# Weight sums pinned to the output projections, and the down projection's seven products in another order

## The chip, the cores and the metric

The kernel runs on one core of one Trainium2 chip. The metric is the device time of one execution in microseconds (us). The engines are TensorE (PE; its weight loads are shown apart as PEld), VectorE (DVE), ScalarE (ACT), GpSimd (POOL) and SyncE (SP). DMA transfers are issued on the queues of SP, ACT and POOL and move through 16 DMA engines that all of them use.

## What is computed

One layer of a streaming encoder on a sequence of 1024 tokens of width 1024, in float32: stick-breaking attention with 16 heads, cross-attention of 4 heads into 256 memory rows, and a gated MLP of width 2816 with a causal convolution over three tokens. Each of the three ends in a projection, a residual and a layer norm:

```python
h = layer_norm(DN_ALPHA * h + mixer(h) @ mix_wo, ln_g[0], ln_b[0])
h = layer_norm(DN_ALPHA * h + mem_cross_attn(h, mem, xa_wq, xa_wkv, xa_wo), ln_g[1], ln_b[1])
# conv_ffn: u = conv(h @ w_up) + b;  g, val = split(u);  (gelu(g) * val) @ w_down
h = layer_norm(DN_ALPHA * h + conv_ffn(h, ffn_up, ffn_conv, ffn_conv_b, ffn_down), ln_g[2], ln_b[2])
```

## The kernel before

Every float32 product is made of three matmuls on operands that are split into a high and a low part (`split`, lines 77 to 87: a cast for the high part, a subtraction for the low one; `mm3`, lines 100 to 103: the three matmuls). A stage's instructions are written in an order, but a scheduler that simulates the program puts each engine's queue into its final order: an instruction that is ready early and has nothing before it in its way can move far to the front of its engine's queue. The queues themselves are then served strictly in order.

The stages are: loading x and projecting the first head (lines 384 to 408), attention head by head with the projections of the next head mixed in (`proj_steps`, `attention`; at the end the keys and values of the memory, `mem_steps`), the first output projection with its layer norm in eight token blocks (`out_ln`, from line 463), cross-attention, the second output projection in the same way, the MLP's up projection with convolution and gate in 22 steps (`late`, `stage1` to `stage3`), and the down projection with the last layer norm (from line 810). In the first stage, `qk_out` (lines 131 to 140) builds head 0's q and k; four transfers q<-q on SP copy halves of q into the tile that the second matmul of the scores, line 216, reads.

Both products of the MLP use a Strassen-like scheme: each operand is cut into 2 x 2 blocks, and seven products of sums of blocks take the place of eight. For the down projection four sums of weight blocks are needed, u1 to u4, each of 11 tiles of 256 KB. They are built in DRAM by transfers alone (`u_steps`, lines 419 to 428): 44 plain copies on SP's queue (line 422) and 44 accumulating transfers on POOL's queue (line 426). The stage's text calls this generator six times after each token block of the first output projection, and six times before each block of the second. Nothing but the copies' own data order holds these transfers to that place. In the projections, the loads of a token block (attention output or h, and the residual) are issued on ACT's queue, a block ahead; SP's queue has the stores of h1 or h2 there (`h_d<-r`, line 488) and loads for what follows. The layer norm's power -0.5 is an instruction on POOL (line 446) between two parts of the norm on DVE.

The last up-projection pair ends with two gates that are stored to DRAM on SP's queue (`gated`, line 738). The down projection loads four quarter tiles ("slots") for each of 11 steps from there (`slot`, line 825, 44 loads `float<-g_d`; two of the eleven steps need the last two gates), and a weight block for each step (`w_block`, line 835). Its products are named 1, 6, 2, 7, 5, 4 and a last one. Each of the first six has 11 steps of 12 matmuls into four PSUM banks; two sets of four banks alternate, so that DVE or ACT empties one while PE fills the other. Sums of slots are made on DVE between the steps. The last product runs row block by row block, 33 matmuls each, and after each of its four blocks two layer norms are done (`finish`), that of a row block in the upper half and that of one in the lower half of the tokens. `layer_norm` has two forms: one on DVE alone, and a spread one (argument `spread`) that uses ACT for the scaling, POOL for the gain and DVE for the offset.

Of the kernel before, what the change touches and what calls it, by code (L numbers as in the profile page):

```python
# [41 lines left out]
def trunk(ctx, tc, out, xT, xn, memT, wqk, wv, wo, xq, xk, xv, xo, up, cw, dn, lng, lnb):  # L42
# [395 lines left out]
    def layer_norm(r, g, b, spread=False):  # L438
        st = smallp.tile([P, 2, 6], F32, name="st")
        for c in range(2):  # L440
            nc.vector.bn_stats(out=st[:, c], in_=r[c])
# [287 lines left out]
    def gated(w, c):  # L729
# [80 lines left out]
    plan = {1: (0, "11"), 6: (0, "u2"), 2: (2, "21"), 7: (None, "u3"), 5: (1, "u1"), 4: (3, "u4")}  # L810
    with ExitStack() as c4:
# [40 lines left out]
        def add(d, x, y):  # L852
            nc.vector.tensor_tensor(out=d, in0=x, in1=y, op=ALU.add)

        def finish(i, spread):
            layer_norm((rs[i][:, 0:512], rs[i][:, 512:1024]), *gb, spread=spread)
# [4 lines left out]
        def factors(m, kt):  # L861

            s, n = plan[m]
            if m == 6:
                nc.vector.tensor_tensor(out=slot(kt, 0), in0=slot(kt, 1), in1=slot(kt, 0), op=ALU.subtract)
            if m == 7:
                x = ea.tile([P, 512], F32, name="sum", bufs=2)
                nc.vector.scalar_tensor_tensor(out=x, in0=slot(kt, 0), scalar=-1.0, in1=slot(kt, 3),
                                               op0=ALU.mult, op1=ALU.subtract)
            else:  # L870
                x = slot(kt, s)
            w = w_block(n, kt)
            a = ea.tile([P, 2, 512], R, name="aop", bufs=4)
            if kt % 2 == 0:
                two["w"] = whlp.tile([P, 2, 2, 512], R, name="whl")
            return (x, (a[:, 0], a[:, 1])), (w, (two["w"][:, kt % 2, 0], two["w"][:, kt % 2, 1]))

        two = {}

        def down(bank, b, a, w, first, last, more):  # L880
# [3 lines left out]
        banks = ([f(name="ya") for f in (acc_tile, acc_tile, pv_tile, pv_tile)],  # L884
                 [f(name="yb") for f in (z_tile, z_tile, tp_tile, tp_tile)])
        last_ops = [[None, None] for _ in range(NH)]
        gb = None
        for n, m in enumerate((1, 6, 2, 7, 5, 4)):
            y = banks[n % 2]
            more = m in (2, 7, 4)  # L890
            if m == 5:
                y = banks[0][:] = [f(name="ya") for f in (acc_tile, acc_tile, pv_tile, pv_tile)]
            for kt in range(NH):
                ops = factors(m, kt)
                for x, d in ops:
                    split(x, *d)
                a, w = ops[0][1], ops[1][1]
                for b in range(4):
                    down(y[b], b, a, w, kt == 0 and not more, kt == NH - 1, more)
                if m == 1:  # L900
                    nc.vector.tensor_tensor(out=slot(kt, 1), in0=slot(kt, 1), in1=slot(kt, 3), op=ALU.subtract)
                if m == 2:
                    add(slot(kt, 2), slot(kt, 2), slot(kt, 0))
                if m == 5:
                    t = w_block("22", kt)
                    wo = room(kt, 0, R), room(kt, 1, R)
                    split(t, *wo)
                    last_ops[kt][1] = wo
                    if 3 <= kt < 7:
                        residual("22", kt - 3, c22[kt - 3], ALU.subtract)  # L910
                if m == 4:
                    vo = room(kt, 3, R), room(kt - 1, 2, R) if kt else ea.tile([P, 512], R, name="vl")
                    split(slot(kt, 2), *vo)
                    last_ops[kt][0] = vo
                    if 3 <= kt < 7:
                        residual("21", kt - 3, c21[kt - 3])
                    elif kt >= 7:
                        residual("12", kt - 7, c12[kt - 7], ALU.subtract)
            if m == 7:
                gb = load_ln(ep, 2)  # L920
            for b in range(4):
                if m == 1:
                    nc.scalar.copy(out=c21[b], in_=y[b])
                elif m == 6:
                    add(c12[b], y[b], c21[b])
                elif m == 2:
                    residual("11", b, y[b])
                elif m == 7:
                    add(c22[b], y[b], c21[b])
                elif m == 5:  # L930
                    add(c22[b], c22[b], y[b])
# [47 lines left out]
```

## Time and profile before

| | us |
|---|---|
| median of 3 runs (1631.63 to 1636.67) | 1632.85 |
| the profiled execution | 1636.42 |
| its span, first to last instruction | 1634.6 |
| PE busy | 1520.0 (93%) |
| DVE busy | 1099.9 (67%) |
| ACT busy | 700.7 (43%) |
| POOL busy | 639.4 (39%) |

All times within the execution count from the span's start. A busy PE is one with a matmul in its pipeline, not one at its peak; the granted clock tells how fast it may run (1.00 is 2.4 GHz, 0.50 is 1.2 GHz). The DMA share is the mean busy share of the 16 DMA engines, and can come out a little over 1. A timeline line reads: start, duration, engine and line, operation, tile written <- tiles read, count, and in brackets the engine's idle time before it with what ended it.

### The profile page before, as it was taken

To read this page: it belongs to the slowest core of one execution; us is meant where nothing else is said; L and a number is where in the kernel's file an instruction comes from. 1 tells how busy PE (TensorE), PEld (TensorE's weight loads), DVE (VectorE), ACT (ScalarE), POOL (GpSimd) and SP (SyncE) were. 2 spreads that over 40 slices of the span, in tenths; PEclk is the share of its full clock that TensorE was granted. 3 is DMA by queue.
4 is the path that set the end of the run, shared out by engine and by line. 5 is a ranking of instruction groups with operands and counts; after the bars stand their busy time and mean duration, and the time that the engine had idled before them with its cause. 6 is when DMAs were issued, how large, how long until landed. Compare 5 with 4: busy or idle time off the path is not lost.

```text
span 1634.6 us, 20991 instructions
## 1 busy us (share of the span) xinstructions
PE 1520.0 (93%) x7508; PEld 1266.1 (77%) x7508; DVE 1099.9 (67%) x1500; ACT 700.7 (43%) x1306; POOL 639.4 (39%) x565
## 2 busy tenths in 40 slices
PE   5639999999998899999999987999999999799996
PEld 4428888888887698888888866788888888588875
DVE  2127566676667974655545789877777777868778
ACT  2315556555556651113332334444444444344551
POOL 4758656655655881035520133233232322000004
PEclk8759999999999999999999999999999999899998
DMA  9975221212223653433326412222222222854532
GB/s 276 258 183 127 71 62 51 76 53 59 65 62 109 194 195 101 133 112 109 110 68 190 142 52 80 91 78 77 80 93 86 78 90 78 283 182 129 187 103 104
DMA packets 99193, 191.01 MB, mean 117 GB/s; under 512 B 11408, under 2 KB 33040, under 8 KB 99088
## 3 DMA queue, kind: packets, MB, share of 16 engines
q1 hardware_dynamic: 84688, 160.30, 30.9%
q0 software_dynamic: 6336, 11.54, 4.0%
q10 hardware_dynamic: 8064, 17.83, 3.3%
q8 instruction: 59, 0.97, 0.2%
q14 instruction: 46, 0.38, 0.1%
HBM read 146.63 MB, written 57.67 MB: 125 GB/s over the span
## 4 chain that ended last, share of the span: by engine, by line
PE 76%; DMA 9%; DVE 9%; issue 2%; POOL 2%; ACT 2%; SPq 0%; DVEq 0%; POOLq 0%; ACTq 0%
DMA u_d<-in_dn 4%; PE yacc L101 4%; PE yacc L102 4%; PE yacc L103 4%; PE mb L101 3%; PE mb L103 3%; PE mb L102 3%; PE tp L231 3%; PE qkacc L101 3%; PE qkacc L102 3%; PE qkacc L103 3%; PE ma L101 2%; PE ma L102 2%; PE ma L103 2%; PE mc L101 2%
## 5 line engine op out<-in xcount | busy, mean ns | idle before, releaser
L222 DVE TENSOR_TENSOR_SCAN sig<-sig 128x896 f32<-128x896 f32 (+7 forms) x128 | 204.2, 1603 | 90.7 <-POOL sig L219 51.4
L87 POOL TENSOR_TENSOR whl<-wraw,whl 128x512 fp32r<-128x512 f32 (+2 forms) x97 | 178.5, 1856 | 155.9 <-ACT whl L79 154.7
L446 POOL TENSOR_TENSOR rs<-rs,mhalf 128x1 f32<-128x1 f32 x24 | 21.3, 890 | 362.4 <-DVE rs L445 362.4
L85 DVE TENSOR_TENSOR wT<-tp,wT 128x512 fp32r<-128x512 f32 (+1 forms) x160 | 99.0, 630 | 67.5 <-ACT wT L79 65.8
L79 ACT CAST wT<-tp 128x512 fp32r<-128x512 f32 (+1 forms) x160 | 86.4, 546 | 106.2 <-PE tp L231 101.4
L79 ACT CAST whl<-wraw 128x512 fp32r<-128x512 f32 (+3 forms) x113 | 82.2, 739 | 108.2 <-PE yacc L103 33.1
L217 ACT ACTIVATE sig<-z 128x384 f32<-128x384 f32 (+2 forms) x192 | 91.8, 495 | 81.6 <-PE z L216 80.8
L101 PE MATMUL qkacc<-xh,whl 128*128 128x512 f32 x256 | 104.9, 410 | 21.8 <-ACT xh L79 19.7
L101 PE MATMUL mb<-b_t,ws 128*128 128x512 f32 x264 | 105.1, 399 | 10.5 <-ACT ws L79 8.1
L103 PE MATMUL qkacc<-xh,whl 128*128 128x512 f32 x256 | 103.2, 403 | 4.6 <-POOL whl L87 4.6
L103 PE MATMUL mb<-b_t,ws 128*128 128x512 f32 x264 | 104.4, 396 | 0.0
L102 PE MATMUL mb<-b_t,ws 128*128 128x512 f32 x264 | 103.8, 393 | 0.0
L102 PE MATMUL qkacc<-xl,whl 128*128 128x512 f32 x256 | 103.7, 405 | 0.0
L219 POOL TENSOR_SCALAR_AFFINE_SELECT sig<-sig 128x128 f32<-128x128 f32 x128 | 58.0, 457 | 114.9 <-ACT sig L217 107.9
L102 PE MATMUL yacc<-wo,whl 128*128 128x512 f32 x256 | 100.9, 394 | 0.0
L103 PE MATMUL yacc<-wo,whl 128*128 128x512 f32 x256 | 100.8, 394 | 0.0
L101 PE MATMUL yacc<-wo,whl 128*128 128x512 f32 x256 | 100.4, 393 | 0.3 <-ACT whl L79 0.3
L216 PE MATMUL z<-k,q 128*128 128x384 f32 (+2 forms) x192 | 68.6, 359 | 31.1 <-DMA q<-q 31.1
L231 PE MATMUL tp<-ident,sig 128*128 128x128 f32 x576 | 89.0, 274 | 8.6 <-DVE wT L85 8.4
L79 ACT CAST ws<-wt 128x512 fp32r<-128x512 f32 x88 | 54.3, 620 | 94.7 <-PE mb L103 52.6
L83 POOL TENSOR_SCALAR whl<-wraw 128x512 fp32r<-128x512 f32 (+2 forms) x74 | 62.3, 871 | 79.8 <-PE q2acc L103 23.1
L85 DVE TENSOR_TENSOR whl<-wraw,whl 128x512 fp32r<-128x512 f32 (+3 forms) x90 | 66.4, 746 | 35.0 <-ACT whl L79 34.8
(225 smaller groups left out, 4435.0 us busy)
## 6 DMA issues: line engine op xcount, KB each, us to landing
u_d<-in_dn SPq DMA_DIRECT2D x44, 256.0 KB, 13.1
wraw<-in_up SPq DMA_DIRECT2D x22, 512.0 KB, 3.7
wr<-in_up SPq DMA_DIRECT2D x22, 512.0 KB, 3.5
g_d<-gate SPq DMA_DIRECT2D x22, 512.0 KB, 2.7
float<-g_d SPq DMA_DIRECT2D x44, 256.0 KB, 5.4
wraw<-u_d SPq DMA_DIRECT2D x44, 256.0 KB, 3.0
wraw<-in_dn SPq DMA_DIRECT2D x33, 256.0 KB, 3.1
q<-q SPq DMA_DIRECT2D x64, 128.0 KB, 2.5
```

The costliest lines, as they stand in the source:

```text
L79: nc.scalar.copy(out=hi, in_=src)
L83: nc.gpsimd.tensor_scalar(out=hi, in0=src, scalar1=1.0, scalar2=0.0, op0=ALU.mult, op1=ALU.add)
L85: nc.vector.tensor_tensor(out=lo, in0=src, in1=hi.bitcast(F32), op=ALU.subtract)
L87: nc.gpsimd.tensor_tensor(out=lo, in0=src, in1=hi.bitcast(F32), op=ALU.subtract)
L101: nc.tensor.matmul(o, lhsT=lh, rhs=rh, start=first, stop=False, skip_group_check=more)
L102: nc.tensor.matmul(o, lhsT=lh, rhs=rl, start=False, stop=False, skip_group_check=more)
L103: nc.tensor.matmul(o, lhsT=ll, rhs=rh, start=False, stop=last, skip_group_check=more)
L216: nc.tensor.matmul(z[:, :b - a], lhsT=q2[:, tb], rhs=k1[:, a:b], start=False, stop=True)
L217: nc.scalar.activation(out=sig[:, a:b], in_=z[:, :b - a], func=AF.Sigmoid, scale=-0.125)
L219: nc.gpsimd.affine_select(out=sig[:, S - P:S], in_=sig[:, S - P:S], pattern=[[-1, P]], base=-1, channel_multiplier=1, compare_op=ALU.is_ge ...
L222: nc.vector.tensor_tensor_scan(out=kr, data0=kr, data1=kr, initial=1.0, op0=ALU.mult, op1=ALU.bypass)
L231: nc.tensor.transpose(out=tp[:, k], in_=sigs[2 * d + u][:, P * j:P * j + P], identity=ident)
```

## The change

The 88 transfers that build the weight sums get an edge each to the instruction that was traced before them on their engine, so that the scheduler can't move them ahead of it. The store of the last pair's two gates goes to POOL's queue. The seven products of the down projection run in the order 1, 6, 5, 7, 4, 3 and last 2. The bank sets are 0, 1, 0, 1, 1, 0 and a new one for the last product; the statistics of each half row for the last layer norm are taken as soon as that half is complete (`whole`), and the layer norms of the lower half of the tokens are done during product 3, leaving four for the last product, all in the spread form.

```diff
     def u_steps():
         for n, x in (("u1", "11"), ("u3", "22"), ("u2", "22"), ("u4", "21")):
             for kt in range(NH):
-                nc.sync.dma_start(out=u_d[n][kt], in_=b_block(x, kt))
+                tc.keep_in_program_order(nc.sync.dma_start(out=u_d[n][kt], in_=b_block(x, kt)))
                 yield
         for n, x in (("u1", "12"), ("u3", "12"), ("u2", "u1"), ("u4", "u2")):
             for kt in range(NH):
-                nc.gpsimd.dma_start(out=u_d[n][kt], in_=u_d[x][kt] if x[0] == "u" else b_block(x, kt),
-                                    accum_op=ALU.add, max_dma_last_dim=2048)
+                tc.keep_in_program_order(nc.gpsimd.dma_start(
+                    out=u_d[n][kt], in_=u_d[x][kt] if x[0] == "u" else b_block(x, kt),
+                    accum_op=ALU.add, max_dma_last_dim=2048))
                 yield
...
-            nc.sync.dma_start(out=g_d[w.j + c], in_=gate[c])
+            (nc.gpsimd if w is pairs[-1] else nc.sync).dma_start(out=g_d[w.j + c], in_=gate[c])
...
-    plan = {1: (0, "11"), 6: (0, "u2"), 2: (2, "21"), 7: (None, "u3"), 5: (1, "u1"), 4: (3, "u4")}
+    plan = {1: (0, "11"), 6: (0, "u2"), 5: (1, "u1"), 7: (1, "u3"), 4: (3, "u4"), 3: (0, "22")}
...
+        def whole(n, b):
+
+            i, ns = rows(n)[b]
+            if i not in stats:
+                stats[i] = ep.tile([P, 2, 6], F32, name=f"st{i}")
+            nc.vector.bn_stats(out=stats[i][:, int(n[1]) - 1], in_=rs[i][:, ns])
...
+        for m, n in ((1, 0), (6, 1), (5, 0), (7, 1), (4, 1), (3, 0)):
+            if m in (1, 6, 5):
+                sets[n] = bank_set(n)
+            y, more = sets[n], m not in (1, 6, 5)
             for kt in range(NH):
...
+                elif m == 5:
+                    nc.vector.scalar_tensor_tensor(out=slot(kt, 1), in0=slot(kt, 0), scalar=-1.0, in1=slot(kt, 3),
+                                                   op0=ALU.mult, op1=ALU.subtract)
+                elif m == 7:
+                    plus(slot(kt, 0), slot(kt, 2), slot(kt, 0))
...
+                elif m == 3:
+                    last_ops[kt][0] = room(kt, 0, R), room(kt - 1, 2, R) if kt else ea.tile([P, 512], R, name="lo2")
+                    split(slot(kt, 2), *last_ops[kt][0])
+                    if kt < 4:
+                        residual("12", kt, c12[kt], ALU.subtract)
+                    if kt in (3, 5, 7, 9):
+                        finish(4 + (kt - 3) // 2, kt != 9)
...
+                elif m == 7:
+                    plus(c22[b], c22[b], y[b], ALU.subtract)
+                    whole("22", b)
+                elif m == 4:
+                    plus(c21[b], c21[b], y[b])
+                    whole("21", b)
                 else:
-                    add(c21[b], c21[b], y[b])
+                    plus(c12[b], c12[b], y[b])
+                    whole("12", b)
+        y = bank_set(1)
         for b in range(4):
             for kt in range(NH):
-                a, w = last_ops[kt]
-                down(banks[0][b], b, a, w, False, kt == NH - 1, True)
-            finish(4 + b, b < 3)
-            add(c12[b], c12[b], banks[0][b])
-            finish(b, b % 2 == 0)
+                down(y[b], b, *last_ops[kt], kt == 0, kt == NH - 1, False)
+            plus(c11[b], c11[b], y[b])
+            whole("11", b)
+            finish(b, True)
```

## Rows read from the trace of the kernel before

**Rows 1.** Table by stages: length, busy us of each engine, clock, DMA share, GB/s.

```profile
26.40:77.40 51.00, 32.06 (x107) 23.77 (x106) 5.53 (x8) 12.18 (x23) 31.07 (x36) 0.73 1.09 267
77.40:108.50 31.10, 0.03 (x1) 0.01 (x1) 0.69 (x1) 2.26 (x4) 9.64 (x12) 0.56 1.01 250
108.50:120.00 11.50, 11.03 (x42) 8.40 (x43) 8.40 (x7) 5.91 (x13) 11.21 (x14) 0.71 0.16 24
120.00:600.00 480.00, 466.05 (x2742) 402.69 (x2741) 342.95 (x372) 278.27 (x609) 316.43 (x318) 0.99 0.32 90
636.00:724.00 88.00, 88.00 (x419) 73.06 (x418) 53.90 (x89) 12.94 (x20) 14.52 (x13) 1.00 0.40 132
858.00:947.00 89.00, 88.73 (x415) 73.10 (x414) 58.41 (x105) 24.34 (x47) 12.12 (x10) 1.00 0.49 158
1531.00:1561.00 30.00, 30.00 (x133) 24.47 (x131) 26.55 (x44) 18.08 (x32) 0.00 (x0) 1.00 0.84 266
```

**Rows 2.** Timeline of PE, 0 to 130 us.

```profile
35.49 0.80 PE L101 MATMUL qkacc<-xh,whl 128*128 128x512 f32 x1 [9.04 <-ACT xh L79]
...
58.73 0.79 PE L103 MATMUL qkacc<-xh,whl 128*128 128x512 f32 x1 [4.63 <-POOL whl L87]
...
76.81 0.39 PE L102 MATMUL vtacc<-xl,whl 128*128 128x512 f32 x1
77.04 0.40 PE L103 MATMUL vtacc<-xh,whl 128*128 128x512 f32 x1
108.53 1.08 PE L216 MATMUL z<-k,q 128*128 128x384 f32 x2 [31.09 <-DMA q<-q]
```

**Rows 3.** Timeline of SP's queue, 0 to 120 us.

```profile
33.59 40.10 SPq L422 DMA_DIRECT2D u_d<-in_dn  x24
...
104.26 1.38 SPq L139 DMA_DIRECT2D q<-q  x2
```

**Rows 4.** The tile u_d's instructions: ns min/median/max, first and last start.

```profile
L422 SPq DMA_DIRECT2D u_d<-in_dn x44: 490/491/1151, 9.6 to 96.9; - x44
...
L426 POOL DMA_DIRECT2D u_d<-in_dn x22: 787/814/1752, 16.4 to 67.8; - x22
L426 POOL DMA_DIRECT2D u_d<-u_d x22: 814/1328/2318, 68.3 to 128.8; - x22
```

**Rows 5.** Timeline of PE where the down projection begins.

```profile
1421.99 0.80 PE L101 MATMUL ya<-whl,aop 128*128 128x512 f32 x1 [9.66 <-ACT aop L79]
```

**Rows 6.** Timeline of PE, its last matmul.

```profile
1621.32 0.39 PE L103 MATMUL ya<-float32r,float32r 128*128 128x512 f32 x1
```

**Rows 7.** Timeline of DVE, the end.

```profile
1626.48 0.68 DVE L853 TENSOR_TENSOR y<-y,ya 128x512 f32<-128x512 f32 x1
...
1630.03 1.41 DVE L460 SCALAR_TENSOR_TENSOR y<-y,rs,lnb 128x512 f32<-128x512 f32 x2
```

**Rows 8.** DMA view, 110 to 150 us: a queue's share; KB, us to landing.

```profile
q0 software_dynamic: 1584, 2.88, 42.6%
...
wraw<-in_wqk SPq DMA_DIRECT2D x2, 512.0 KB, 4.3
```

**Rows 9.** Timeline of POOL, second output projection.

```profile
884.19 0.99 POOL L446 TENSOR_TENSOR rs<-rs,mhalf 128x1 f32<-128x1 f32 x1 [44.97 <-DVE rs L445]
```

**Rows 10.** DMA issues of the whole page: KB each, median us to landing.

```profile
wraw<-in_wqk SPq DMA_DIRECT2D x15, 512.0 KB, 3.7
```

**Rows 11.** Timeline of SP's queue at the same place as rows 5.

```profile
1413.64 0.38 SPq L835 DMA_DIRECT2D wraw<-u_d  x1
1416.99 0.33 SPq L738 DMA_DIRECT2D g_d<-gate  x1
1417.41 15.39 SPq L825 DMA_DIRECT2D float<-g_d  x22
```

**Rows 12.** The tile y's instructions: ns min/median/max, first and last start.

```profile
L452 ACT ACTIVATE y<-y,nm,rs x10: 798/806/817, 1599.3 to 1622.6; 128x512 f32<-128x512 f32 x10
L453 POOL TENSOR_TENSOR y<-y,lng x10: 1288/1332/1742, 1600.2 to 1624.3; 128x512 f32<-128x512 f32 x10
```

More of the change, by code (lines that the diff above doesn't have):

```diff
@@ L436, in load_ln, with layer_norm @@
         return g, b
[L438 to L441, printed above, removed]
+    def layer_norm(r, g, b, spread=False, st=None):
+        if st is None:
+            st = smallp.tile([P, 2, 6], F32, name="st")
+            for c in range(2):
+                nc.vector.bn_stats(out=st[:, c], in_=r[c])
         mv = smallp.tile([P, 2], F32, name="mv")
@@ L850, in residual, with plus @@
             nc.vector.scalar_tensor_tensor(out=quarters[n][b], in0=t, scalar=ALPHA, in1=x, op0=ALU.mult, op1=op)
-        def add(d, x, y):
-            nc.vector.tensor_tensor(out=d, in0=x, in1=y, op=ALU.add)
+        def plus(d, x, y, op=ALU.add):
+            nc.vector.tensor_tensor(out=d, in0=x, in1=y, op=op)
+        stats = {}
+        def whole(n, b):
[3 more added lines that the diff above has]
+            nc.vector.bn_stats(out=stats[i][:, int(n[1]) - 1], in_=rs[i][:, ns])
         def finish(i, spread):
-            layer_norm((rs[i][:, 0:512], rs[i][:, 512:1024]), *gb, spread=spread)
+            layer_norm((rs[i][:, 0:512], rs[i][:, 512:1024]), *gb, spread=spread, st=stats[i])
             for n in range(2):
@@ L859, in finish, with w_ops @@
                 (nc.scalar if n else nc.sync).dma_start(out=out[i, :, ns], in_=rs[i][:, ns])
[L861 to L873, printed above, removed]
+        two = {}
+        def w_ops(kt):
             if kt % 2 == 0:
                 two["w"] = whlp.tile([P, 2, 2, 512], R, name="whl")
-            return (x, (a[:, 0], a[:, 1])), (w, (two["w"][:, kt % 2, 0], two["w"][:, kt % 2, 1]))
-        two = {}
+            return two["w"][:, kt % 2, 0], two["w"][:, kt % 2, 1]
         def down(bank, b, a, w, first, last, more):
@@ L882, in down, with bank_set @@
             mm3(bank, a[0][:, bb], a[1][:, bb], w[0], w[1], first, last, more)
-        banks = ([f(name="ya") for f in (acc_tile, acc_tile, pv_tile, pv_tile)],
-                 [f(name="yb") for f in (z_tile, z_tile, tp_tile, tp_tile)])
+        def bank_set(n):
+            return [f(name="y") for f in ((z_tile, z_tile, tp_tile, tp_tile) if n == 0 else
+                                                           (acc_tile, acc_tile, pv_tile, pv_tile))]
         last_ops = [[None, None] for _ in range(NH)]
+        sets = {}
         gb = None
[L888 to L892, printed above, removed]
-            for kt in range(NH):
[L894 to L897, printed above, removed]
+        for m, n in ((1, 0), (6, 1), (5, 0), (7, 1), (4, 1), (3, 0)):
+            if m in (1, 6, 5):
+                sets[n] = bank_set(n)
+            y, more = sets[n], m not in (1, 6, 5)
+            for kt in range(NH):
+                s, u = plan[m]
+                x, t = slot(kt, s), ea.tile([P, 2, 512], R, name="aop", bufs=4)
+                if m == 6:
+                    plus(x, slot(kt, 1), x, ALU.subtract)
+                a, w = (t[:, 0], t[:, 1]), w_ops(kt)
+                split(x, *a)
+                split(w_block(u, kt), *w)
                 for b in range(4):
@@ L900, in trunk @@
                 if m == 1:
[L901 to L908, printed above, removed]
-                    if 3 <= kt < 7:
[L910 to L914, printed above, removed]
+                    plus(slot(kt, 1), slot(kt, 1), slot(kt, 3), ALU.subtract)
+                elif m == 5:
[3 more added lines that the diff above has]
+                    plus(slot(kt, 0), slot(kt, 2), slot(kt, 0))
+                    if 3 <= kt < 7:
+                        plus(c22[kt - 3], c22[kt - 3], c21[kt - 3], ALU.subtract)
+                    elif kt >= 7:
+                        residual("11", kt - 7, c21[kt - 7])
+                elif m == 4:
+                    last_ops[kt][1] = room(kt, 1, R), room(kt, 3, R)
+                    split(w_block("21", kt), *last_ops[kt][1])
                     if 3 <= kt < 7:
                         residual("21", kt - 3, c21[kt - 3])
-                    elif kt >= 7:
-                        residual("12", kt - 7, c12[kt - 7], ALU.subtract)
-            if m == 7:
+                elif m == 3:
[5 more added lines that the diff above has]
+                        finish(4 + (kt - 3) // 2, kt != 9)
+            if m == 5:
                 gb = load_ln(ep, 2)
```

10 lines of the change are left out of this document (4 added, 6 removed).

## The prediction

> **What bounds the kernel now.** I read the table by stages first [rows 1]: TensorE (PE) is busy in 88.00 of 88 us of the first output projection, in 88.73 of 89 of the second and in 466.05 of 480 of the attention. Time can therefore be had only where PE stands still or runs slowly, and the table shows where: before 120 us. From 26.40 to 77.40 PE is busy 32.06 of 51.00 us at a granted clock of 0.73, and from 77.40 to 108.50 it does nothing, while the DMA engines are full (share 1.09 and 1.01). PE's own timeline names the releasers [rows 2]: 9.04 us of idle until ScalarE has split a piece of x, 4.63 us until a weight split on GpSimd, and 31.09 us until the transfer q<-q. SyncE's queue shows why that transfer is late [rows 3]: 24 copies u_d<-in_dn hold the queue for 40.10 us from 33.59, and the last two q<-q go out at 104.26. So the 88 transfers that build the weights' sums, of which only the down projection at the kernel's end has need, run at its very front [rows 4]: 44 copies between 9.6 and 96.9 us, 44 accumulations between 16.4 and 128.8. Two places at the end cost PE less: at the join of the two MLP products it stands 9.66 us [rows 5], and after its last matmul at 1621.32 the vector engine (DVE) works until 1631.4 [rows 6, 7].
>
> **The change part by part.** The profiled execution took 1636.42 us, 1.8 us of it outside its span of 1634.6 and 3.6 us over the median of 1632.85. I sum against the execution and take the result off the median.
>
> *The pins, at the front.* They put an edge from each of the 88 transfers to the instruction traced before it on its queue. The 44 copies go behind h1_d's stores of the first projection, six per token block and two after the last; four accumulations follow there, and forty go to the second projection. Out of the front comes: the 31.09 us of idle; of the 18.9 us of idle from 26.40 to 77.40 (51.00 - 32.06) the 12.3 that are waits for loads, since 6.6 are waits for other work, the largest 4.63 for a split on GpSimd [rows 2]; and slow matmuls: 107 in 32.06 us are 0.300 each, where two starts at full speed lie 0.23 apart (76.81 and 77.04), so 107 x 0.07 = 7.5. After 108.5 PE starts at clock 0.71 for 11.5 us [rows 1]; I take 2 of the 3.2 us (11.03 x 0.29) that this costs. Sum 31.1 + 12.3 + 7.5 + 2 = 53. Low end: the idle alone, 43. High end: these 6.6 as well, since u_d issues of 0.8 us and more on its queue [rows 4] go from among its splits too: 60. I take 53, because GpSimd's splits also stand behind the subtractions for q and k, which stay. As PE is busy 97% of the attention, the shift should go through to the end.
>
> *The pins, at their new place.* The DMA work: 44 copies of 256 KB at the 250 GB/s of the full engines [rows 1] are 46 us; 11 accumulations held 42.6% of 40 us [rows 8], 1.55 us each, so 44 are 68 us, measured under crowding. Free are 0.60 x 88 = 53 us in the first projection and 0.51 x 89 = 45 in the second [rows 1], and the stretch before it, as its first six accumulations hang only on GpSimd's last split of the cross-attention, after which it is idle for 44.97 us [rows 9]. So it fits, barely. Behind the copies on SyncE wait h1_d's next store, the xq weights and, at the stage's end, kraw. The projections' own loads are issued on ScalarE's queue, one block ahead. What a load pays beside accumulations has a row: in_wqk landed after 4.3 us there [rows 8], against 3.7 over the kernel [rows 10]. On GpSimd the power of a layer norm is queued behind up to six issues, 6 x 0.81 = 4.9 us at the least and 6 x 1.33 = 8.0 by the median [rows 4]; powers come a block apart, 89 / 8 = 11.1 us in the mean, so they collide only where two blocks close together. An accumulation waits itself for the copy or sum that it adds to, issued a block or more earlier. Price 0 to 12, I take +2.
>
> Here a rule speaks against the change. Row first: issuing u_d<-u_d took 814 to 2318 ns, median 1328 [rows 4], in a stretch that begins with DVE busy 8.40 of 11.50 us [rows 1]. The Trainium skill (SBUF — State Buffer, "SBUF: two separate sides") says that GpSimd cannot write a transfer's descriptors while DVE holds the port pair they share, and its next section has a transfer of 0.62 us take 3.1 in that case. By that figure 40 issues would be an estimated 124 us, 35 more than the 89 of the second projection. The rows don't reach it; with their worst value it is the second rival.
>
> *Last gates stored by GpSimd.* On SyncE 22 loads of the down projection (float<-g_d) stand behind the last g_d store, which waits for DVE until 1416.99 [rows 11]; PE stands 9.66 us for the first of them [rows 5]. With the store gone the queue is free after its u_d load at 1413.64, at 1413.96: 3.45 us earlier. What stands before that in the queue, weight blocks, follows PE's pace and stays. I take -4, with the first slow matmuls. Were the 22 loads moved up to the end of the MLP's last product they could save all 9.66 and some 2 of slow matmuls, -12; were they held by the stored tiles themselves, each store's issue of 0.8 us on GpSimd [rows 4] instead of 0.33 on SyncE [rows 11], with a later landing, costs up to +2. On GpSimd nothing is queued behind these two stores until the layer norms.
>
> *The other order.* All seven products remain, 132 matmuls each. New is that the fourth and the fifth share a bank set: the fifth's first matmul of a bank waits for DVE's sum out of it, an operation of 0.68 us [rows 7], while PE has the other three banks, 9 matmuls of 0.23 or 2.1 us; 0 to +2, I take +1. Half the layer norms move from the last product into the sixth. DVE needs 26.55 us for 44 operations there, 0.60 each [rows 1]. The sixth gets 33 splits, 4 residuals, 8 operations that close the fifth, and four layer norms of 1.6 to 3.0: 45 x 0.60 + 7.8 = 34.8 us against 30 of PE. DVE may run up to four steps of 2.7 us ahead, and the last product asks little of it. Cost 0 to +6, I take +2.
>
> *The tail.* The last sum starts at 1626.48, 4.8 us after PE could release it, because DVE is full of earlier layer norms; from there to the end of its last operation are 5.0 us [rows 7]. After the change this queue is short, but the last block takes the spread form: sum, statistics and scalars 1.8, power 1.0, nm 0.2, one ACT pass 0.81, two GpSimd products of 1.33 [rows 12] and a DVE sum 0.68 [rows 7], with gaps 8.2. 4.8 + 5.0 - 8.2 = 1.6 gained; 0 to 5.
>
> Sum: -53 + 2 - 4 + 1 + 2 - 1.6 = -53.6: 1582.8 for the execution, 1579 on the median.
>
> **The rivals.** (1) The join comes free entirely: 8 us more, 1571. For it: nothing in the code ties these loads to the gates. Against it: they were put behind the last store in that queue [rows 11], as if their room came free late. (2) GpSimd bounds the second projection: with 2.318 us an issue, six and a power of 0.99 are 14.9 us a block against 89 / 8 = 11.1, some 21 us over its 5.7 blocks, 1600. Against it: the median. The rule above, where this would come from, is not borne out so far. (3) The front's gain stays partial: with q early, PE waits instead for the first chain of scores, sigmoid, scan and transposes, or a re-made plan of the attention is poorer; 31 of the 53 come, 1601. Against it: the second head's projection, at PE from 58.73 to 77.04 [rows 2], is other work to fill that chain. (4) Slower: the sums' transfers are not hidden but stand ahead of the projections' own. They are 46 + 68 = 114 us of full engines; it decides from 47% exposed (53.6 of 114). With two thirds, 76, the time is 1655. For it: the room is used up, and on a shared queue q<-q waited for copies. Against it: the 4.3 us, and that the loads have another queue. The Trainium skill (DMA: Bandwidth & Descriptors, "Queues, rings and completion order") has every DMA engine take turns between queues, by which this rival falls; no row shows ScalarE's queue beside copies. (5) The pins don't hold the copies: the front stays, only join, order and tail act, 1632.
>
> **How the numbers follow.** Chances: forecast 0.58, (1) 0.14, (2) 0.12, (3) 0.08, (4) 0.05, (5) 0.03. The forecast's own spread is 1566 to 1592. The extremes of all terms are -77 (60 + 12 + 5) and -21 (-43 + 2 + 12 + 6 + 2), 1556 and 1612. For 8 in 10 the range goes from 1558 to 1604: it holds the forecast and the rivals (1) to (3) but for their edges. A measurement of this kernel tells some 0.3%, 5 us, from no change. Faster: 0.58 + 0.14 + 0.12 + 0.08 = 0.92; the same: 0.03; slower: 0.05.
>
> **What would show it.** Right: no u_d transfer before 600 us, q<-q landing in 3 us, the first scores' second matmul near 50 to 57 us, PE still 88 of 88 us in the projections with the DMA share near 0.9, float<-g_d issued without a g_d store ahead, DVE's last sum within 1 us of PE's end. Wrong: PE idle in the projections with ACT's splits waiting for loads, powers queued for many us behind u_d issues, a gap in front of the attention that remains, or DVE full in the sixth product with PE waiting.

## The result, and the profile after

The changed kernel takes 1593.59 us (median of 4 runs, 1591.35 to 1596.7), the one before 1632.72 beside it: a ratio of 0.9757, 95% interval 0.9734 to 0.9781, so 39 us faster. A later comparison of the same two gave 0.9726 (0.9712 to 0.9741). The forecast was 1579, with a range of 1558 to 1604: direction and range hold, the gain is some 9 to 15 us short, by which of the two ratios, or of the medians, it is taken. The profiled execution took 1592.65 us, its span 1590.9.

The stages first, as in [rows 1] (length, busy us of PE, PE's weight loads, DVE, ACT, POOL, granted clock, DMA share, GB/s), of the changed kernel:

```profile
26.40:48.30 21.90, 20.02 (x79) 14.94 (x79) 4.72 (x8) 9.17 (x19) 13.21 (x14) 0.92 0.28 84
60.00:540.00 480.00, 467.21 (x2742) 404.41 (x2741) 339.35 (x375) 280.71 (x615) 305.62 (x312) 0.99 0.29 84
578.00:666.00 88.00, 88.00 (x420) 73.04 (x418) 54.33 (x90) 12.68 (x20) 17.18 (x15) 1.00 0.81 252
800.00:820.00 20.00, 17.49 (x77) 13.73 (x76) 5.56 (x16) 6.67 (x16) 0.00 (x0) 0.91 0.50 149
840.00:860.00 20.00, 17.75 (x79) 14.14 (x78) 12.50 (x23) 5.28 (x10) 9.22 (x11) 0.91 1.10 260
880.00:900.00 20.00, 18.32 (x84) 14.71 (x83) 12.85 (x21) 3.46 (x5) 9.84 (x10) 1.00 0.92 215
1517.00:1547.00 30.00, 29.00 (x128) 23.50 (x126) 30.00 (x50) 17.98 (x31) 13.15 (x10) 1.00 0.35 119
```

The hole of the front is gone: the scores' second matmul, at 108.53 in [rows 2], starts at 48.74, and the attention runs as before. The first projection carries its 44 copies at a DMA share of 0.81 with PE at 88.00 of 88. The second projection does not carry its accumulations: where PE was busy 88.73 of 89 us, three windows of 20 us now lose 2.51, 2.25 and 1.68 us, two of them at a clock of 0.91.

Two lines of PE's last matmuls of a tile (count, ns min/median/max, first and last start) cut the run into stages; first of the kernel before, then of the changed one:

```profile
L103 PE MATMUL q2acc<-h1h,whl x128: 387/389/477, 713.3 to 845.0; 128*128 128x512 f32 x128
L103 PE MATMUL yacc<-wo,whl x256: 388/392/482, 619.2 to 949.4; 128*128 128x512 f32 x128
```

```profile
L103 PE MATMUL q2acc<-h1h,whl x128: 387/389/497, 655.9 to 786.9; 128*128 128x512 f32 x128
L103 PE MATMUL yacc<-wo,whl x256: 388/392/628, 561.7 to 905.1; 128*128 128x512 f32 x128
```

At the cross-attention's last query matmul the changed kernel is 845.0 - 786.9 = 58.1 us ahead, at the last matmul of the second projection 949.4 - 905.1 = 44.3. From there the distances to the first matmul of the down projection, to PE's last one and to the end of the span are read in the same way. The table has them for every run of this study, in us; A to E add up to the span:

| kernel | A: to last query matmul | B: to last of second projection | C: to first of down projection | D: to PE's last | E: to the end | span | ratio (interval) |
|---|---|---|---|---|---|---|---|
| before | 845.0 | 104.4 | 443.5 | 228.4 | 13.3 | 1634.6 | 1 |
| changed | 786.9 | 118.2 | 440.3 | 234.3 | 11.2 | 1590.9 | 0.9757 (0.9734 to 0.9781) |
| changed, again | 788.1 | 118.2 | 440.4 | 234.1 | 11.2 | 1592.0 | 0.9726 (0.9712 to 0.9741) |
| pins alone | 789.3 | 117.7 | 439.7 | 231.4 | 13.5 | 1591.6 | 0.9717 (0.9696 to 0.9739) |
| no accumulations | 790.7 | 104.5 | 441.8 | 231.9 | 11.1 | 1580.0 | 0.9669 (0.9651 to 0.9687) |
| accumulations in the up projection | 785.8 | 104.4 | 441.9 | 231.9 | 11.2 | 1575.2 | 0.9661 (0.9644 to 0.9678) |
| residuals kept in place | 787.1 | 117.5 | 442.0 | 228.2 | 11.9 | 1586.7 | 0.9716 (0.9702 to 0.9731) |
| narrow accumulations | 781.6 | 110.7 | 439.7 | 230.1 | 11.1 | 1573.2 | 0.9673 (0.9654 to 0.9693) |
| gates on SyncE | 788.7 | 118.6 | 440.0 | 231.8 | 11.0 | 1590.1 | 0.9735 (0.972 to 0.975) |
| up projection and residuals | 785.1 | 104.5 | 443.0 | 226.5 | 11.8 | 1570.9 | 0.9613 (0.9599 to 0.9626) |
| the same, gates first | 786.5 | 104.5 | 440.9 | 227.9 | 11.8 | 1571.6 | 0.9613 (0.9598 to 0.9628) |
| the same, products 1 and 6 mixed | 786.1 | 104.5 | 441.8 | 219.7 | 11.9 | 1564.0 | 0.9588 (0.9575 to 0.9601) |
| no pins | 844.5 | 104.5 | 443.0 | 235.5 | 11.1 | 1638.6 | 1.0005 (0.9995 to 1.0014) |

B tells most: 118 us within 0.6 wherever the full accumulations lie in it, 110.7 with narrow ones, 104.4 to 104.5 wherever there are none. The cut between A and B moves a little: wherever accumulations lie in B, full or narrow, twelve score matmuls and four transposes of the cross-attention stand behind the last query matmul (787.15 to 789.00 in the changed kernel), and ahead of it elsewhere. So of B's +13.8 some 11.9 are lost time, and of A's -58.1 some -56.2 are the front. A is no fine measure besides: in the eleven executions with pins it lies between 781.6 and 790.7, though their edits all lie behind the attention. What moves it is not settled, and such differences in A are not read as effects. C and D are read together where the order of the last stage differs, since the first matmul of the down projection is mixed into the end of the up projection. From before to changed: A -58.1, B +13.8, C and D +2.7, E -2.1, in sum -43.7. Ratios come from four comparisons, each with runs of the kernel before beside it; the changed kernel's own two differ by 0.003, so differences below some 5 us between lines are read from stages, not from medians.

### The profile page after: what moved, and what is told of

Same layout as the page of the kernel before. It is cut to its first block, busy times and chain, and to the rows that moved or that the text cites. A ratio compares the mean times of both kernels' runs of the same rounds, so it can differ in the third digit from the quotient of the medians.

```text
span 1590.9 us, 20977 instructions
## 1 busy us (share of the span) xinstructions
PE 1521.3 (96%) x7508; PEld 1267.0 (80%) x7508; DVE 1100.6 (69%) x1502; ACT 703.9 (44%) x1310; POOL 643.4 (40%) x571
## 4 chain that ended last, share of the span: by engine, by line
PE 72%; DVE 10%; DMA 8%; POOL 4%; issue 4%; ACT 2%; SPq 1%; DVEq 0%; ACTq 0%; POOLq 0%
PE qkacc L101 4%; PE qkacc L103 3%; PE qkacc L102 3%; PE tp L231 3%; PE mb L101 3%; PE mb L103 3%; PE mb L102 3%; PE y L102 3%; PE y L103 3%; PE y L101 3%; PE ma L103 2%; PE ma L101 2%; PE ma L102 2%; PE mc L101 2%; PE mc L102 2%
## 5 line engine op out<-in xcount | busy, mean ns | idle before, releaser
L222 DVE TENSOR_TENSOR_SCAN sig<-sig 128x896 f32<-128x896 f32 (+7 forms) x128 | 196.8, 1544 | 73.9 <-POOL sig L219 55.2
L87 POOL TENSOR_TENSOR whl<-wraw,whl 128x512 fp32r<-128x512 f32 (+2 forms) x97 | 173.9, 1804 | 144.4 <-ACT whl L79 142.8
L102 PE MATMUL y<-whl,aop 128*128 128x512 f32 x264 | 104.4, 397 | 1.6 <-DVE whl L85 1.6
L103 PE MATMUL y<-whl,aop 128*128 128x512 f32 x264 | 101.4, 396 | 0.0
L101 PE MATMUL y<-whl,aop 128*128 128x512 f32 x264 | 85.5, 398 | 12.3 <-ACT aop L79 7.6
```

The costliest lines, as they stand in the source:

```text
L87: nc.gpsimd.tensor_tensor(out=lo, in0=src, in1=hi.bitcast(F32), op=ALU.subtract)
L101: nc.tensor.matmul(o, lhsT=lh, rhs=rh, start=first, stop=False, skip_group_check=more)
L102: nc.tensor.matmul(o, lhsT=lh, rhs=rl, start=False, stop=False, skip_group_check=more)
L103: nc.tensor.matmul(o, lhsT=ll, rhs=rh, start=False, stop=last, skip_group_check=more)
L222: nc.vector.tensor_tensor_scan(out=kr, data0=kr, data1=kr, initial=1.0, op0=ALU.mult, op1=ALU.bypass)
```

## The experiments

**Part against part: the pins alone.** The kernel before with the two pins of `u_steps` and nothing else.

> The kernel before with the 88 pins alone: old order of the products, gates on SyncE, old tail. Theory 1 (from the two traces side by side: the changed kernel is 47.5 us ahead when the down projection begins and 43.7 at the end of the span, so the other three edits together lose 3.8): 1593.6 - 3.8 = 1589.8. Theory 2 (the prediction's terms for join, order and tail, -4 + 1 + 2 - 1.6 = -2.6, hold and all of the shortfall lies with the pins): 1593.6 + 2.6 = 1596.

1588.63 us, 0.9717. Theory 1: the pins bring all of the gain. What the other three edits do, C + D + E, is 684.6 us with the pins alone, 685.2 before, 685.8 in the changed kernel.

**The other parts alone.** The changed kernel without its pins.

> The changed kernel without its 88 pins: the last two gates, the order of the products and the tail alone. Theory 1 (from the traces: join 2.2 us gained, the shared bank set 6.7 lost, the tail 2 gained): the kernel before plus 1 to 4, ratio 1.000 to 1.0025. Theory 2 (the prediction's terms, -4 + 1 + 2 - 1.6): 2.6 less, ratio 0.9984.

1635.2 us beside 1634.61: 1.0005, within 0.9995 and 1.0014. No difference that can be measured; the forecast's 0.9984 lies outside, and theory 1 holds at its low end. (The profiled execution, span 1638.6, was above its median, so the 4.4 us of its stages C, D and E overstate the loss.) The old front is back in its trace, 32.32 us of idle for q<-q included, so the hole hangs on the pins alone.

**Second projection: the accumulations taken out.** The yield stays, the issue goes.

```diff
-                tc.keep_in_program_order(nc.gpsimd.dma_start(
-                    out=u_d[n][kt], in_=u_d[x][kt] if x[0] == "u" else b_block(x, kt),
-                    accum_op=ALU.add, max_dma_last_dim=2048))
                 yield
```

> The changed kernel without the 44 accumulating transfers; the 44 copies stay (the weight sums are therefore not formed, the rest is as it is). Theory 1 (the accumulations take the 13 us that are lost between the last matmul of the cross-attention's queries, 58.1 us ahead, and the last one of the second projection, 44.3 ahead; some 3 of it come back at the start of the MLP anyway): 1580 to 1584. Theory 2 (the loss belongs to the new order of work there, or to the front's gain running into a chain that was hidden; the accumulations are covered): 1592 to 1595.

1579.39 us, 0.9669, just below theory 1's range, and B falls from 118.2 to 104.5. All of B's 13.8 us come with the accumulations; the copies, which stay, cost B nothing.

**The same transfers at another place.** The six calls ahead of each block of the second projection go; three follow each step of the up projection.

```diff
         for i in range(NTB):
-            for _ in range(6):
-                next(u_sums, None)
             out_ln(i, i, o2_d, wts2, h1_d, rp, gb, h2_d, h2_evac, first_products if i == NTB - 1 else None)
...
         stage3(w)
+        for _ in range(3):
+            next(u_sums, None)
     early2(pairs[-1])
```

> The changed kernel with the 44 accumulations issued three at a time behind each step of the up projection in place of six at a time before each block of the second output projection. The DMA share there is 0.22 to 0.29 and GpSimd is busy 14 to 15 of 50 us. Theory 1 (crowding in the second projection is what costs): the second projection comes as near to 58 us ahead as without the sums, and the up projection has room: 1580 to 1585. Theory 2 (44 issues cost GpSimd and DVE the same anywhere, because they hold each other up): 1590 to 1596, the loss spread over the up projection's steps.

1578.29 us, 0.9661, B 104.4: theory 1, 2 us below its range. In the up projection the transfers are free: C is 441.9 us with them and 441.8 without any. Here are 270 us of it, with 41 of the 44 accumulations in them:

```profile
980.00:1250.00 270.00, 270.00 (x1174) 219.99 (x1173) 204.57 (x239) 121.36 (x156) 110.78 (x83) 1.00 0.49 123
```

PE is busy 270.00 of 270 us although the DMA share is twice that of the changed kernel in its own 270 us from 995 (0.25). The issues themselves (the tile u_d; ns min/median/max, first and last start) take 1.42 us at most, beside a DVE that is busy 204.57 of the 270; in the kernel before [rows 4] the longest took 2.32:

```profile
L426 POOL DMA_DIRECT2D u_d<-in_dn x22: 782/1088/1421, 976.2 to 1110.4; - x22
L426 POOL DMA_DIRECT2D u_d<-u_d x22: 788/1094/1414, 1111.0 to 1247.1; - x22
```

**Bytes or issues?** Each accumulation moves 8 columns of 512.

```diff
-                    out=u_d[n][kt], in_=u_d[x][kt] if x[0] == "u" else b_block(x, kt),
+                    out=u_d[n][kt][:, 0:8], in_=(u_d[x][kt] if x[0] == "u" else b_block(x, kt))[:, 0:8],
```

> The changed kernel with each of the 44 accumulations cut to 8 of its 512 columns, at the same place: as many issues on GpSimd, each still of 128 rows, but 1/64 of the bytes (the weight sums are therefore formed in those columns alone). Theory 1 (what costs in the second projection is the engines' time: residual loads r<-h_d land after 6.9 us in place of 3.0, the DMA share is 1.10): as without the sums, 0.966 of the kernel before or 1579 to 1582. Theory 2 (GpSimd: issues of 1.1 to 1.4 us queued ahead of the layer norms' powers; two of them lasted 2.38 us): 1590 to 1594, with PE still waiting some 6 us for r in the second projection.

1582.08 us, 0.9673: by the median theory 1, at the edge of its range. By stages it is a little over half of a yes: B is 110.7, so 7.5 of the 13.7 us hang on the bytes; 6.2 stay. (The profiled execution, 1575.0, lies 7 us below the median, most of it in A, so only the stages behind A are read here; C and D are 3.9 shorter in it than without accumulations.) The DMA view of the second projection (KB each, median us from issue to landing) tells how, first the changed kernel, then the one with narrow accumulations:

```profile
u_d<-u_d POOLq DMA_DIRECT2D x22, 256.0 KB, 10.8
r<-h_d ACTq DMA_DIRECT2D x16, 256.0 KB, 6.9
h_d<-r SPq DMA_DIRECT2D x14, 256.0 KB, 6.8
u_d<-in_dn POOLq DMA_DIRECT2D x12, 256.0 KB, 14.3
```

```profile
r<-h_d ACTq DMA_DIRECT2D x16, 256.0 KB, 3.2
h_d<-r SPq DMA_DIRECT2D x14, 256.0 KB, 2.9
```

The residual r, which needs 3.0 us in the kernel before, lands after 6.9 beside full accumulations and after 3.2 beside narrow ones. Three waits in PE's timeline of the changed kernel show what comes of that and what doesn't:

```profile
805.37 0.41 PE L560 MATMUL tpp<-ident,p 128*128 128x128 f32 x2 [1.44 <-DVE p L557]
...
853.91 0.63 PE L493 MATMUL tp<-ident,r 128*128 128x128 f32 x4 [2.09 <-DVE r L462]
...
895.89 1.29 PE L493 MATMUL tp<-ident,r 128*128 128x128 f32 x8 [1.65 <-DVE r L462]
```

The second is the load's: DVE's first operation of that block waits 3.22 us for r. The third is GpSimd's: the power of the norm is queued behind six issues and DVE waits for the power. DVE's and POOL's timelines:

```profile
846.81 0.69 DVE L486 SCALAR_TENSOR_TENSOR r<-r,yacc 128x512 f32<-128x512 f32 x1 [3.22 <-DMA r<-h_d]
...
892.89 3.52 DVE L462 SCALAR_TENSOR_TENSOR r<-r,rs,lnb 128x512 f32<-128x512 f32 x2 [3.08 <-POOL rs L448]
```

```profile
887.22 5.04 POOL L426 DMA_DIRECT2D u_d<-u_d  x6
890.47 2.38 POOL L448 TENSOR_TENSOR rs<-rs,mhalf 128x1 f32<-128x1 f32 x1
```

With narrow accumulations PE waits for r nowhere in B; the power's waits behind issues are still there, 3.3 us in two, but with the loads in time PE has work meanwhile. The first wait stays, and it is another matter: 20 us around it are busy 17.50 us at a clock of 0.91 there, 17.49 at 0.91 in the changed kernel, and 19.69 at 1.00 with the accumulations in the up projection. No accumulation is issued in the changed kernel between those around 768 and those from 832; what differs is how the cross-attention's last blocks and the projection's first are interleaved; the twelve score matmuls that stand later are part of that. That this goes with accumulations traced at this place is shown, full or narrow; the calls of `u_steps` alone don't do it, as they are still there without accumulations, where B is 104.5. Why the order comes out poorer is not settled. The 6.2 us are nearly all named: 1.9 of work moved over the cut, 2.1 of idle more than without accumulations (2.5 against 0.4), and an estimated 1.8 of slow matmuls (20 us at 0.91).

**The bank boundary: residuals kept in place.** In the changed kernel PE stands between products 7 and 4, which share a bank set. PE's timeline there, and DVE's:

```profile
1480.84 0.39 PE L103 MATMUL y<-whl,aop 128*128 128x512 f32 x1
1485.96 0.76 PE L101 MATMUL y<-whl,aop 128*128 128x512 f32 x1 [4.74 <-DVE y L855]
1486.52 0.63 PE L102 MATMUL y<-whl,aop 128*128 128x512 f32 x1
```

```profile
1476.88 0.69 DVE L852 SCALAR_TENSOR_TENSOR y<-h2r,y 128x512 f32<-128x512 f32 x1 [2.19 <-DMA h2r<-h_d]
...
1483.93 0.69 DVE L852 SCALAR_TENSOR_TENSOR y<-h2r,y 128x512 f32<-128x512 f32 x1
1484.53 0.68 DVE L85 TENSOR_TENSOR whl<-wraw,whl 128x512 fp32r<-128x512 f32 x1
1485.13 0.68 DVE L855 TENSOR_TENSOR y<-y,y 128x512 f32<-128x512 f32 x1
```

The first sum out of the set is not long, 0.68 us; it stands in DVE's queue behind residual operations of later steps, which the scheduler has moved ahead and which wait for their loads. All sixteen residual operations of the stage have run before it. After the stop ten matmuls run 0.43 us apart in place of 0.23.

```diff
-            nc.vector.scalar_tensor_tensor(out=quarters[n][b], in0=t, ...)
+            s = nc.vector.scalar_tensor_tensor(out=quarters[n][b], in0=t, ...)
+            if n == "21":
+                tc.keep_in_program_order(s)
```

> The changed kernel with the four residual operations of quarter 21 kept behind the operation traced before them on DVE, so that they can't stand ahead of the sums that empty the bank set shared by the fourth and fifth product. Theory 1 (DVE is late at that boundary because these operations wait for their loads h2r; PE stands 4.74 us there and runs 10 matmuls at 0.43 us in place of 0.23): both go, 1593.6 - 6.7 = 1587. Theory 2 (DVE is short of time in products 7 and 4 as a whole, so the four operations are late elsewhere and stall the sixth product): 1592 to 1594, a wait of some us near the last steps of the fifth or sixth product.

1586.88 us, 0.9716. Eight residual operations now run behind the sums, the four of quarter 21 and four that follow them. The stall is gone, and no wait of over 1.1 us takes its place in the down projection but that of the join; on DVE the sum now follows the splits directly:

```profile
1480.58 0.69 DVE L85 TENSOR_TENSOR float32r<-wraw,float32r 128x512 fp32r<-128x512 f32 x1 [1.42 <-ACT float32r L79]
1481.19 0.69 DVE L85 TENSOR_TENSOR whl<-wraw,whl 128x512 fp32r<-128x512 f32 x1
1481.79 0.68 DVE L857 TENSOR_TENSOR y<-y,y 128x512 f32<-128x512 f32 x1
```

D is 6.1 us shorter, as theory 1 has it; with C and E, which are 2.4 longer, 3.7 remain. By the ratios it is 1.6 to 6.7, by which comparison of the changed kernel it is held against.

**The join: the gates' store put back on SyncE.**

```diff
-            (nc.gpsimd if w is pairs[-1] else nc.sync).dma_start(out=g_d[w.j + c], in_=gate[c])
+            nc.sync.dma_start(out=g_d[w.j + c], in_=gate[c])
```

> The changed kernel with the last two gates stored by SyncE's queue, as before the change. Theory 1 (the loads float<-g_d of steps 5 to 10 take room that is free only when DVE's last gate operation has ended; the first went out at 1368.55, that operation ended at 1367.30 + 1.22 = 1368.52; the store ahead of them was never the cause): one issue of 0.33 us and its gap later, 1594.0 to 1594.4, no difference that can be measured. Theory 2 (the prediction's term for the join: the store in SyncE's queue holds them): 4 us slower, 1597.6.

1592.74 us beside 1592.07, 0.9735 against 0.9726: theory 1. In the changed kernel the end of DVE's last gate operation (L739) and the first load of the sixth step meet, with no store in the queue; these are DVE's, SyncE's and PE's timelines:

```profile
1367.30 1.22 DVE L739 TENSOR_TENSOR gate<-gate,cv 128x1024 f32<-128x1024 f32 x1
```

```profile
1365.00 0.66 SPq L837 DMA_DIRECT2D wraw<-u_d  x1
1368.55 11.28 SPq L827 DMA_DIRECT2D float<-g_d  x17
```

```profile
1372.28 0.80 PE L101 MATMUL y<-whl,aop 128*128 128x512 f32 x1 [7.42 <-ACT aop L79]
```

1367.30 + 1.22 = 1368.52, and the load goes out at 1368.55, though SyncE was free from 1365.66. With the store on SyncE it is this instead:

```profile
1370.30 0.33 SPq L740 DMA_DIRECT2D g_d<-gate  x1
1370.68 5.75 SPq L827 DMA_DIRECT2D float<-g_d  x10
```

The store holds the issue up by 0.38 us. PE pays more than that: its first matmul of the step starts 4.88 us after the first load's issue, where it was 3.73, and it stands 8.80 us where it was 7.42 (7.28 in the second trace of the changed kernel):

```profile
1375.56 0.79 PE L101 MATMUL y<-whl,aop 128*128 128x512 f32 x1 [8.80 <-ACT aop L79]
```

So some 1.4 of the 4 us of the prediction's term are there as idle of PE. The total shows no difference.

**Both repairs.** The accumulations in the up projection and the residuals in place, together.

> The changed kernel with the accumulations in the up projection and the residual operations of quarter 21 kept in their traced place, both. Theory 1 (two separate losses, they add): 1578.3 less the stall of 3.66 us that the first of the two still shows at the bank boundary and about 1 of slow matmuls, 1573 to 1574. Theory 2 (the residual operations only move their wait, now that PE comes earlier to them): 1577 to 1579.

1572.19 us, 0.9613: they add, theory 1, 1 us below its range. B is 104.5, and D 226.5 where it was 231.9 with the first repair alone. The two losses have separate places.

**The join again: gate operations first.** On top of that, product 1's subtractions are traced and kept in product 6.

```diff
                 if m == 6:
+                    tc.keep_in_program_order(plus(slot(kt, 1), slot(kt, 1), slot(kt, 3), ALU.subtract))
                     plus(x, slot(kt, 1), x, ALU.subtract)
...
                 if m == 1:
-                    plus(slot(kt, 1), slot(kt, 1), slot(kt, 3), ALU.subtract)
+                    slot(kt, 1), slot(kt, 3)
```

> As the one before, and the eleven subtractions of slots 1 and 3 that DVE makes during product 1 are traced and kept in product 6, one ahead of each step's own subtraction, so that DVE's last gate operations have no subtractions ahead of them. Theory 1 (DVE's last gate operation ends the join's wait; some 18 subtractions of 0.6 us, 11 us, stand between the up projection's last matmul and it): PE's 7.3 us of idle at step 5 of product 1 shrink to 0 to 2, with the slow restart 6 to 9 us, so 1565 to 1568. Theory 2 (DVE lacks the time: with two subtractions and two splits, 2.4 us a step of 2.7, product 6 stalls instead, or the loads themselves keep PE waiting): 1571 to 1575.

1573.26 us, 0.9613 again: theory 1 falls. The time lies in theory 2's range, but no other wait of PE over 1.0 us has come into the down projection, so DVE isn't short of time in product 6. No subtraction stands ahead of the gates any more, and PE still waits 6.68 us. PE's, DVE's and SyncE's timelines:

```profile
1344.39 0.39 PE L103 MATMUL mb<-b_t,ws 128*128 128x512 f32 x1
...
1358.05 0.80 PE L101 MATMUL y<-whl,aop 128*128 128x512 f32 x1 [6.68 <-ACT aop L79]
```

```profile
1345.97 0.69 DVE L657 TENSOR_TENSOR u<-mb,ms 128x512 f32<-128x512 f32 x1
1347.97 1.28 DVE L726 SCALAR_TENSOR_TENSOR cv<-u,cws,cv 128x1024 f32<-128x1024 f32 x1 [1.32 <-ACT cv L724]
...
1351.75 1.22 DVE L737 TENSOR_TENSOR gate<-gate,cv 128x1024 f32<-128x1024 f32 x1
```

```profile
1353.00 13.83 SPq L827 DMA_DIRECT2D float<-g_d  x18
```

The chain starts at the up projection's last matmul, which stands at 1344.39, among the first steps of product 1: combine, convolution, gate to 1352.97, loads from 1353.00, and 5 us later the sixth step's first matmul. DVE being busy with subtractions added little to it. So PE has to have other work for that long.

**Products 1 and 6 mixed.** Steps 0 to 4 of product 6, whose slots are loaded already, go between steps 4 and 5 of product 1.

```diff
-        for m, n in ((1, 0), (6, 1), (5, 0), (7, 1), (4, 1), (3, 0)):
+        lo, hi, full = range(5), range(5, NH), range(NH)
+        for m, n, kts in ((1, 0, lo), (6, 1, lo), (1, 0, hi), (6, 1, hi), (5, 0, full), (7, 1, full), (4, 1, full),
+                          (3, 0, full)):
...
-            for kt in range(NH):
+            for kt in kts:
```

> The kernel with the accumulations in the up projection and the residual operations in their place (0.9613 of the kernel before), in which products 1 and 6 are mixed: steps 0 to 4 of product 1, steps 0 to 4 of product 6, then 5 to 10 of each. Theory 1 (at the join PE has only the five steps whose loads don't take the up projection's room; the chain from the last up-projection matmul over combine, convolution, gate and a load of 4.3 us to the sixth step is what it waits for, and the five steps of product 6, 5 x 2.7 = 13.6 us, cover it): the 7.2 us of idle and about 2 of slow restart go, 1563 to 1566 or 0.956. Theory 2 (the sums' weights or the loads behind them in SyncE's queue are late as well, so the wait moves): 1570 to 1574, 0.960 to 0.962.

1566.02 us, 0.9588, where its base had 0.9613: by the time the edge of theory 1's range, by the ratio between its 0.956 and theory 2's 0.960. The trace decides for theory 1. The join's idle is gone; the granted clock stays at 1.00 (level 2.4 GHz) through it:

```profile
1345.00:1355.00 10.00, 10.00 (x45) 8.27 (x45) 10.00 (x13) 4.57 (x7) 0.64 (x1) 1.00 0.32 106
1355.00:1365.00 10.00, 10.00 (x45) 8.28 (x45) 6.30 (x9) 3.73 (x7) 0.54 (x1) 1.00 0.69 234
1365.00:1375.00 10.00, 9.94 (x44) 7.90 (x43) 8.92 (x14) 3.53 (x6) 0.00 (x0) 1.00 1.03 373
```

C and D together are 661.5 us in place of 669.5, the 8 that theory 1 asks for; the ratios make it 0.0025 or 4 us, the two medians 6. One wait of 1.27 us for a weight split is new. This version is the fastest of the study, 26 to 28 us below the changed kernel's medians.

## Why the prediction was right, and where it was short

*The front* was right, and rather more than right. The steps that it named show: no u_d transfer before 578.8, q<-q landing after 2.2 us (median of the page), the scores at 48.74 where 50 to 57 was said. A is 58.1 us shorter, some 56.2 without the work that moved over the cut, against 53 with a high end of 60; A's spread of 9 us doesn't tell these apart. The traces show what the middle value left out: of the 6.6 us of idle that [rows 2] put down to waits for other work most went too, the 4.63 for GpSimd's split to 0.86, now that no u_d issue [rows 4] stands among its splits. From 26.40 to 48.30 PE stands 1.88 us in all. Rival (3), a front that gives only 31, and rival (5) fell here; the run without pins shows what (5) would have looked like.

*The pins at their new place* are the step that failed. The prediction took 2 us, between 0 and 12; stage B pays 13.8, some 11.9 of it lost time, and it is the accumulations alone. 7.5 of it hang on their bytes. The copies' part held: 88.00 of 88. Two things in the working were wrong. First the sum was made over the stage: 68 us of accumulations into 45 us of free engines and the stretch before "fits, barely". But they go out six at a time, and six by 1.55 us are 9.3 us of full engines in each block of 11 us, just when its r is under way; the share from 840 to 880 is 1.10. Second the price of a load beside accumulations was taken from the row that was there, 4.3 us for in_wqk [rows 8], where the accumulations' queue q0 held 42.6% of the engines; from 840 to 880 it holds 73.1%, and r lands after 7.0 us (median of seven). With r 0.2 us later than in the kernel before (narrow accumulations) PE waits for it nowhere in B; with r 3.9 us later PE stands 2.09 us at the transposes. The prediction also had no term for an order of the cross-attention's end that comes out poorer. Rival (4), transfers not hidden, is what happened, in a small part: some 12 of its 114 us. Of rival (2) there is one trace, the 3.08 us at 892.89 behind issues of 0.84 us each; the issues of the changed kernel have a median of 1.1 to 1.4 us and a longest of 2.95, and GpSimd bounds no stage. The row behind this rival was read amiss: of the 22 issues u_d<-u_d in [rows 4] eleven, the 2.318 among them, start between 68.3 and 86.9, where DVE hardly works (0.69 us from 66 to 108.5). Beside a busy DVE stood only the eleven from 117.0, median 1.348, longest 1.973; the first eleven have a median of 0.814. What makes the later ones longer was not tried. Two slips change nothing: SyncE's queue would be free at 1413.64 + 0.38 = 1414.02, not 1413.96, and rival (5) is 1630 by its own terms, not 1632.

The Trainium skill (SBUF — State Buffer, "SBUF: two separate sides" and the section after it) has GpSimd's transfers go from 0.62 to 3.1 us where DVE holds the port pair. No run here shows such a step, though the rows are issues and the figure is a transfer's: 44 issues have a median of 1.09 us in the up projection, where DVE is busy 204.57 of 270 us. The page ties the lock-out of the descriptors to DVE's two-port modes, and DVE's work there is operations with two inputs; whether that is the reason was not tried. Its rule on arbitration (DMA: Bandwidth & Descriptors, "Queues, rings and completion order"), that an engine takes turns between queues, is not contradicted: r on ACT's queue lands after 6.9 us, later than the 3.0 without accumulations but ahead of the 10.8 to 14.3 of those that it stands beside.

*The join* was judged by the wrong wait. The prediction read the order in SyncE's queue, loads behind a store [rows 11], as the cause, and wrote the likely one down as a doubt: that the loads' room might come free late. Put back, the store costs 0.38 us at the issue, some 1.4 us of PE's idle and no measurable time. In the two traces shown without the store the loads go out 0.03 us after the last gate operation on DVE, and ahead of that lies the chain from PE's last up-projection matmul; that it is the room which this operation sets free is read from these times, not tested by itself. Rival (1), a free join, needed another edit, the mixed products. It is worth 8 us by stages, 4 to 6 by ratio and medians, where the rival had 12 in all.

*The same bank set* was mis-sized: +1, at most 2, and 4.74 us of idle with about 2 us of slow matmuls came. The working counted the length of one DVE operation and not its place in DVE's queue; the kernel's own residuals were in front of it. The bound of 2 us held only if nothing else stood there.

*DVE in product 3* and *the tail* came as forecast. DVE is full, 30.00 of 30 us, and PE stands 1.58 us at 1547.59, near its end, against +2. The last sum starts at 1580.15, 0.4 us after PE's last matmul starts, and E is 2.1 us shorter, against 1.6. DVE's timeline of the changed kernel:

```profile
1580.15 0.69 DVE L855 TENSOR_TENSOR y<-y,y 128x512 f32<-128x512 f32 x1 [0.16 <-PE y L103]
```

So of the four parts one carries the gain. Join, order (DVE's price with it) and tail were forecast at -2.6 together, and no difference can be measured (+0.8 us, -0.8 to +2.3). The total missed its middle value by the loss in B and at the bank boundary, of which a front some 3 us better than its middle value covered a part.

## What to carry to other kernels

Transfers that are due only at the end belong where the DMA share is low for long, spread thin, and not where a stage's mean share still has room for them: price them by the burst that stands beside one load, against how far ahead that load is issued. A loaded queue's order shows what waits, not what it waits for: compare the moment of release with the ends of all engines' work before moving an instruction off the queue. And where two products share a bank set, price the operation that empties it by what stands ahead of it in its engine's queue, its own length being the least of it.

## What was not expected of the hardware

Accumulating transfers issued by GpSimd ran with DVE 76% busy at 0.8 to 1.4 us an issue, and 41 of them beside 270 us of the up projection cost PE nothing, at twice the DMA share (0.49 against 0.25). Narrow accumulations, 4 KB in place of 256, took GpSimd no less time to issue: 1.43 to 1.74 us in the median against 1.11 to 1.42.
